# Recurrent gates of an RG-LRU layer: three products of 64 rows each in place of two products of 128 stacked rows

## The chip, the cores and the metric

The kernel runs on one NeuronCore of a Trainium2 chip. TensorE (PE) multiplies matrices and writes PSUM. VectorE (DVE), ScalarE (ACT) and GpSimd (POOL) do elementwise work, and SyncE (SP) issues most transfers. The metric is the device time of one execution in microseconds (us), lower is better, and it is given as the median of several runs. For the kernel before it is 686.44 us, the median of 3 runs from 683.94 to 686.56.

## The reference, cut to what matters

One encoder layer on x of shape (1, 1024, 1024), float32: an input LayerNorm, one wide input projection, neighbourhood attention, a bidirectional RG-LRU recurrence, gated merging of the two branches, an output projection, and a last LayerNorm. The change is in the gates of the recurrence. There, `w_gate` holds one 64 x 64 matrix for each of 8 channel blocks and each of the two gates r and i, and each of the two directions has its own set.

```python
u = centred_depthwise_conv(u, conv_w, conv_b)                 # (1, 1024, 512)
h = rg_lru(u, gate_w[0], gate_b[0], lam[0], False) + rg_lru(u, gate_w[1], gate_b[1], lam[1], True)

def rg_lru(x, w_gate, b_gate, lam, reverse):
    xb = x.reshape(B, S, N_BLOCKS_B, BLOCK_W)                 # 8 blocks x 64
    g = jnp.einsum('bsnd,gnde->gbsne', xb, w_gate) + b_gate[:, None, None]
    g = jax.nn.sigmoid(g.astype(jnp.float32)).reshape(2, B, S, W)
    r_gate, i_gate = g[0], g[1]
    log_a = -C_LRU * jax.nn.softplus(-lam.astype(jnp.float32)) * r_gate
    a = jnp.exp(log_a)
    ...
    bx = mult * i_gate * x.astype(jnp.float32)
    _, h = lax.associative_scan(_lin_combine, (a, bx), axis=1, reverse=reverse)
```

## The kernel before

**Split precision.** Matmul operands are in the type float32r. To keep float32 accuracy, an operand f is split into a high part (`hi`, f cast to float32r) and a low part (`lo = f - hi`, `lo_of`, line 119). A product is then the sum of high x high, low x high and high x low (`mm3`, line 122): three matmuls, each with its own weight load.

**The stages.** After LayerNorm, the v and q projections, the main loop (line 973) runs over slots: 16 pairs of column tiles of the input projection, 7 slots for each pair, 116 slots with the tail. `product(p, k)` puts one slot's 24 multiplications of a Strassen-like scheme on TensorE: 128 x 128 weights, 128 x 512 moving data. In about the 145th to the 372nd us the recurrence is laid into this loop. Attention follows, then the merge and the output projection.

**Who sets the order.** The order on all engines is the program order: TensorE's is written by hand, and `tc.manual_schedule` (line 141) fixes that of the other four. Within a slot, work registered with `at(slot, 0, f)` is issued before `product`, and that of `at(slot, 1, f)` after it. `CONV_AT` (line 32) gives the first slot of each of the 4 channel tiles' convolution, `GATE_AT` (line 33) that of each of the 8 gate stages (channel tile t, direction d).

**The convolution stage** (`conv_stage`, line 675) makes a channel tile's `uc`: 128 channels, which are two blocks of 64, by 1024 positions. It also loads that tile's gate weights (`w_gate`, line 681), casts them (`weights`, line 700, ACT) and makes their low part (`weights_lo`, line 704, POOL). `split(b)` and `split_lo(b)` (lines 689 and 695) build one stacked operand for each block b: in `us[b]` one half of the 128 rows is the high part of the block's 64 channels (ACT), and the other half their low part (DVE). The host lays the 64 weight rows of a block out twice, once for each half.

**The gate stage** (`gate_stage`, line 718). `gates(b)` (line 721) makes both gates of block b over all 1024 positions, 64 output columns each: for each of the two halves of the positions one matmul with the high weights and one with the low weights. As the rows are stacked, these two give all four products of high and low parts. So a stage has 8 matmuls, and the 8 stages have 64. The result fills `o`, two PSUM banks, one for each half of the positions; the pool `psd` has one such buffer, so that `gates(1)`, two slots later, writes where the sigmoids of `gates(0)` have read. `sigmoid(b, c)` (line 732, ACT) reads 64 x 1024 from PSUM, two for each `gates` call, one slot after it. Then follow the gated input on POOL (line 739), exp, tanh, square and root on ACT, the scan on DVE.

Of the kernel before, what the change touches and what calls it, by code (L numbers as in the profile page):

```python
# [9 lines left out]
F32 = mybir.dt.float32  # L10
F32R = mybir.dt.float32r
AF = mybir.ActivationFunctionType
ALU = mybir.AluOpType

P = 128
S = 1024
# [6 lines left out]
HALF = 512  # L23
# [23 lines left out]
HALVES = ((slice(0, 64), slice(64, P)), (slice(64, P), slice(0, 64)))  # L47
# [8 lines left out]
def tiled(ap, n):  # L56

    return ap[:, n * HALF:(n + 1) * HALF].rearrange("p (j r c) -> p j r c", r=GR, c=8)


def gridded(ap, n):

    return ap.rearrange("p (r j c) -> p j r c", r=GR, c=8)[:, 4 * n:4 * n + 4]
# [3 lines left out]
def encoder_kernel(ctx, tc, x, gb1, gb, w_qk, w_v, w_s, w_ba, w_bb, w_gate, smalls, bias, w_out, out):  # L67
    nc = tc.nc
    V, A, G, PE, SP = nc.vector, nc.scalar, nc.gpsimd, nc.tensor, nc.sync

    def pool(name, side="left", **kw):
        return tc.alloc_tile_pool(name=name, bufs=1, side=side, reuse_waits="tile", **kw)
# [11 lines left out]
    def bank(name):  # L84
        return banks[0].tile([P, HALF], F32, tag="bank", name=name)
# [21 lines left out]
    sm = cst.tile([P, SM_N], F32, name="sm")  # L107

    def pair(pl, shape, name, **kw):
        return [pl.tile(shape, F32R, name=f"{name}_{c}", **({**kw, "tag": kw["tag"] + c} if "tag" in kw else kw))  # L110
                for c in "hl"]
# [7 lines left out]
    def lo_of(eng, lo, full, hi):  # L119
        eng.tensor_tensor(lo, full, hi.bitcast(F32), ALU.subtract)  # L120
# [70 lines left out]
    halves = [slice(c * HALF, (c + 1) * HALF) for c in range(2)]  # L191
# [394 lines left out]
    psd = tc.alloc_tile_pool(name="psd", bufs=1, space=bass.MemoryType.PSUM, reuse_waits="tile")  # L586
# [3 lines left out]
    ev = pool("ev", "right")  # L590
    lru = pool("lru", "right")
# [22 lines left out]
    ups, ucs, hsum = {}, {}, {}  # L614
# [57 lines left out]
    def at(slot, pos, f):  # L672
        todo.setdefault((slot, pos), []).append(f)

    def conv_stage(t, slot):
        cw = SM_CW + 4 * t

        def begin():
            uc = lru.tile([P, S], F32, tag="uc", bufs=2, name=f"uc{t}")
            gs = ev.tile([P, 4, P], F32, tag="z", bufs=5, name=f"gw{t}")  # L680
            SP.dma_start(gs[:], w_gate[t])
            ucs[t] = [uc, [None, None], None, gs]
            A.activation(uc[:], ups[t][:, 0:S], AF.Identity, bias=sm[:, SM_CB + t:SM_CB + t + 1], scale=sm[:, cw:cw + 1])

        def tap(j):
            uc = ucs[t][0]
            V.scalar_tensor_tensor(uc[:], ups[t][:, j:j + S], sm[:, cw + j:cw + j + 1], uc[:], ALU.mult, ALU.add)  # L687

        def split(b):
            uc, us = ucs[t][:2]  # L690
            own, other = HALVES[b]
            us[b] = lru.tile([P, S], F32R, tag=f"us{b}", name=f"us{t}_{b}")
            A.copy(us[b][own], uc[own])

        def split_lo(b):
            uc, us = ucs[t][:2]
            own, other = HALVES[b]
            lo_of(V, us[b][other], uc[own], us[b][own])

        def weights():  # L700
            gw = ucs[t][2] = pair(lru, [P, 4, P], f"gw{t}", tag="gw")
            A.copy(gw[0][:], ucs[t][3][:])

        def weights_lo():
            hi, lo = ucs[t][2]
            lo_of(G, lo[:], ucs[t][3][:], hi[:])

        at(slot, 1, begin)
        for j in range(1, 4):
            at(slot + j, 1, lambda j=j: tap(j))  # L710
        at(slot + 2, 1, weights)
        at(slot + 3, 1, weights_lo)
        at(slot + 5, 1, lambda: split(0))
        at(slot + 6, 0, lambda: split_lo(0))
        at(slot + 6, 1, lambda: split(1))
        at(slot + 7, 0, lambda: split_lo(1))

    def gate_stage(t, d, slot):
        g = {}

        def gates(b):
            uc, us, gw, _ = ucs[t]
            if b == 0:
                for c in "ria":
                    g[c] = lru.tile([P, S], F32, tag=c, name=f"{c}{t}_{d}")
            o = psd.tile([P, 2, HALF], F32, tag="gates", name=f"g{t}{d}{b}")
            for n in range(2):
                for z, w in enumerate(gw):
                    PE.matmul(o[:, n, :], w[:, 2 * d + b, :], us[b][:, n * HALF:(n + 1) * HALF], start=z == 0, stop=z == 1)  # L729
            g["o"] = o[:].rearrange("p n f -> p (n f)")  # L730

        def sigmoid(b, c):
            own, other = HALVES[b]
            src = own if c == "r" else other
            col = SM_GB + (d * 2 + b) * 4 + t
            A.activation(g[c][own], g["o"][src], AF.Sigmoid, bias=sm[src, col:col + 1])

        def gated_input():
            G.tensor_tensor(g["i"][:], g["i"][:], ucs[t][0][:], ALU.mult)

        def decay():
            A.activation(g["a"][:], g["r"][:], AF.Exp, scale=nsp[:, d * 4 + t:d * 4 + t + 1])

        def growth():
            w = g["w"] = lru.tile([P, S], F32, tag="wh", bufs=2, name=f"w{t}_{d}")
            A.activation(w[:], g["r"][:], AF.Tanh, scale=sp[:, d * 4 + t:d * 4 + t + 1])

        def square():
            A.activation(g["r"][:], g["a"][:], AF.Square)

        def left():
            V.scalar_tensor_tensor(g["w"][:], g["r"][:], 1.0, g["w"][:], ALU.add, ALU.mult)

        def root():
            A.activation(g["w"][:], g["w"][:], AF.Sqrt)

        def tables():
            A.activation(warm[:], eps_t[:], AF.Sigmoid)

        def inputs():  # L760
            first = S - 1 if d else 0
            V.memset(g["w"][:, first:first + 1], 1.0)
            G.tensor_tensor(g["w"][:], g["i"][:], g["w"][:], ALU.mult)

        def scan():
            st = -1 if d else 1
            w = g["w"]
            V.tensor_tensor_scan(w[:, ::st], g["a"][:, ::st], w[:, ::st], 0.0, ALU.mult, ALU.add)
            if d == 0:
                hsum[t] = w  # L770

        def fetch():
            for n in range(2):
                zs = g["out", n] = ev.tile([P, HALF], F32, tag="z", bufs=5, name=f"zs{t}_{n}")
                SP.dma_start(zs[:], zb_d[t][:, n * HALF:(n + 1) * HALF])

        def total():
            V.tensor_tensor(hsum[t][:], g["w"][:], hsum[t][:], ALU.add)

        def gated(n):  # L780
            zs = g["out", n]
            V.tensor_tensor(tiled(zs[:], 0), gridded(hsum[t][:], n), tiled(zs[:], 0), ALU.mult)
            SP.dma_start(yb_d[t][:, n * HALF:(n + 1) * HALF], zs[:])

        for b in range(2):
            at(slot + 2 * b, 1, lambda b=b: gates(b))
            for c in "ri":
                at(slot + 2 * b + 1, 1, lambda b=b, c=c: sigmoid(b, c))
        at(slot + 4, 0, gated_input)
        at(slot + 4, 1, decay)  # L790
        at(slot + 5, 1, growth)
        at(slot + 6, 1, square)
        at(slot + 7, 1, left)
        at(slot + 8, 1, root)
        at(slot + 9, 0, tables)
        at(slot + 9, 0, inputs)
        at(slot + 10, 1, scan)
        if d:
            at(slot + 10, 1, fetch)
            at(slot + 11, 1, total)  # L800
            for n in range(2):
                at(slot + 12 + n, 0, lambda n=n: gated(n))
# [74 lines left out]
    for t, slot in enumerate(CONV_AT):  # L877
        conv_stage(t, slot)
    for n, slot in enumerate(GATE_AT):
        gate_stage(n // 2, n % 2, slot)  # L880
# [92 lines left out]
    for slot in range(7 * N_PAIR + 4):  # L973
        p, k = divmod(slot, 7)
# [44 lines left out]
    vvs, sums, scs, tps, pts, attns, rsb, gates = {}, {}, {}, {}, {}, {}, {}, {}  # L1019
# [125 lines left out]
    for unit in range(-NT, H * NT + PV_LAG):  # L1145
        h, c = divmod(unit, NT)
        before, b = divmod(unit - 1, NT)
# [83 lines left out]
    for slot in range(2 * NK + 2):  # L1231
        j, n = divmod(slot, 2)
# [12 lines left out]
        if j < NK:  # L1245
# [3 lines left out]
            o = sums_m[slot] = pst.tile([P, HALF], F32, tag="mb", bufs=2, name=f"mb0{n}") if slot < 2 else bank(f"mb{j}{n}")  # L1249
# [32 lines left out]
    def o_product(i, cols):  # L1282
        o = bank(f"o{i}_{cols.start}")
        w = cols.stop - cols.start
        run(mm3(o[:, :w], [([t[k, i // 4][:, ti(i)] for t in (mh, ml)], [t[:, cols] for t in wo[k]])
                           for k in range(NK)]))
        return o[:, :w]
# [19 lines left out]
    for i in range(NT):  # L1307
        last = i == NT - 1
        load_z(i + 3)
        z = zs.pop(i)  # L1310
# [3 lines left out]
        for cols in [halves[0]] + (pieces[2:] if last else [halves[1]]):  # L1314
            o = o_product(i, cols)
# [110 lines left out]
```

## Time and profile before

| what | value |
|---|---|
| median of 3 runs | 686.44 us (683.94 to 686.56) |
| the profiled execution, its own time | 684.15 us |
| its span, first to last instruction | 682.4 us |
| mean granted TensorE clock | 0.996 |
| HBM read, written | 77.11 MB, 35.68 MB |

The profile shows one execution. A row of a group of instructions has the line in the kernel, the engine, the operation, output and inputs by the program's names, the shape, the count, the busy time in us and the mean of one in ns, and at its end the engine's idle time ahead of these instructions with what ended most of it. PE is the matmul, PEld the weight load, which overlaps it. The end of a matmul is modelled, so its duration is longer than the distance from its start to the next one's start; that distance is called its pitch below. In shapes, 128*64 would be 128 rows by 64 columns of weights, and 128x512 is the moving data.

### The profile page before, as it was taken

How to read it: one execution, taken by the hardware profiler on the slowest of the kernel's cores; microseconds unless marked ns; L12 is line 12 of the kernel's file. 1: busy time of each engine (PE TensorE's matmuls, PEld its weight loads, DVE VectorE, ACT ScalarE, POOL GpSimd, SP SyncE). 2: the span in 40 equal slices, each digit the busy share in tenths (PEclk: the TensorE clock that was granted, in tenths of full speed). 3: DMA queues.
4: the chain of work that ended last, by engine and by line, in shares of the span. 5: the costliest groups of instructions: out<-in, count | busy, mean ns of one | idle time of the engine just before them, and what ended most of it. 6: DMA issues, size and time to landing. Idle time of an engine off the chain costs nothing.

```text
span 682.4 us, 9299 instructions
## 1 busy us (share of the span) xinstructions
PE 666.3 (98%) x3177; PEld 555.0 (81%) x3177; DVE 495.0 (73%) x821; ACT 364.0 (53%) x612; POOL 353.8 (52%) x258
## 2 busy tenths in 40 slices
PE   8999999999999999999999999999999999999995
PEld 6787888888888888888788888888888878888884
DVE  7866766796899599879977785377788777533434
ACT  4553524247686677768576635477777544310110
POOL 5697451344576577567647534115255446435442
PEclk9999999999999999999999999999999999999998
DMA  8754164233424133531453457898794557512211
GB/s 314 241 187 154 63 233 169 78 92 124 124 93 147 68 109 110 183 124 47 170 198 114 174 175 262 293 371 304 257 322 141 179 192 279 183 62 93 92 62 61
DMA packets 48702, 113.39 MB, mean 166 GB/s; under 512 B 5056, under 2 KB 9744, under 8 KB 47120
## 3 DMA queue, kind: packets, MB, share of 16 engines
q1 hardware_dynamic: 48624, 112.81, 47.6%
q8 instruction: 25, 0.41, 0.2%
q14 instruction: 21, 0.17, 0.1%
q10 hardware_dynamic: 32, 0.01, 0.0%
HBM read 77.11 MB, written 35.68 MB: 165 GB/s over the span
## 4 chain that ended last, share of the span: by engine, by line
PE 81%; DVE 8%; DMA 4%; POOL 3%; ACT 1%; issue 1%; SPq 1%; DVEq 0%; POOLq 0%; ACTq 0%
PE a L126 29%; PE o L126 13%; PE s L126 11%; PE mb L126 10%; PE q L126 5%; PE acc L1077 3%; PE s L1031 3%; PE pt L1053 2%; POOL x L238 2%; PE v L303 2%; PE g L729 2%; DMA wvsl<-in_w_v_dram 1%; DMA ks<-k_d 1%; DVE ws_l L120 1%; DVE uc L687 1%
## 5 line engine op out<-in xcount | busy, mean ns | idle before, releaser
L126 PE MATMUL o<-wo_h,ml 128*128 128x512 f32 (+1 forms) x136 | 51.2, 377 | 0.0
L126 PE MATMUL o<-wo_l,mh 128*128 128x512 f32 (+1 forms) x136 | 51.2, 376 | 0.0
L126 PE MATMUL o<-wo_h,mh 128*128 128x512 f32 (+1 forms) x136 | 51.2, 376 | 0.0
L126 PE MATMUL a<-ht_h,ws_h 128*128 128x512 f32 x128 | 50.0, 390 | 0.0
L126 PE MATMUL a<-ht_h,ws_l 128*128 128x512 f32 x128 | 49.8, 389 | 0.0
L126 PE MATMUL a<-ht_l,ws_h 128*128 128x512 f32 x128 | 49.8, 389 | 0.0
L126 PE MATMUL a<-b_h,wa_h 128*128 128x512 f32 x128 | 49.8, 389 | 0.0
L126 PE MATMUL a<-b_h,wa_l 128*128 128x512 f32 x128 | 49.8, 389 | 0.0
L126 PE MATMUL a<-b_l,wa_h 128*128 128x512 f32 x128 | 49.8, 389 | 0.0
L1041 DVE CUSTOM_DVE_ANT_0 sc<-s,bias 128x384 f32<-128x384 f32 (+1 forms) x64 | 33.4, 522 | 22.4 <-PE s L1031 14.0
L1316 DVE SCALAR_TENSOR_TENSOR z<-z,o 128x512 f32<-128x512 f32 (+1 forms) x17 | 11.2, 656 | 51.1 <-PE o L126 51.1
L1061 ACT CAST pt_h<-pt 128x384 fp32r<-128x384 f32 x64 | 29.0, 454 | 25.8 <-PE pt L1053 17.9
L1326 POOL TENSOR_TENSOR z<-z,gb 128x1024 f32<-128x1024 f32 x7 | 16.8, 2396 | 48.7 <-ACT z L1325 48.7
L1046 ACT ACTIVATE p<-sc,summ 128x384 f32<-128x384 f32 (+1 forms) x64 | 37.8, 591 | 5.2 <-DVE summ L1041 5.0
L1295 ACT ACTIVATE sd<-mv,eps_z 128x1 f32<-128x1 f32 x8 | 2.4, 294 | 67.1 <-DVE mv L1321 67.1
L303 PE MATMUL v<-wv,b_h 128*128 128x512 f32 x128 | 32.8, 398 | 2.7 <-ACT b_h L258 1.6
L120 DVE TENSOR_TENSOR pt_l<-pt,pt_h 128x384 fp32r<-128x384 f32 x64 | 33.2, 519 | 2.1 <-ACT pt_h L1061 1.6
L1031 PE MATMUL s<-ks,qs 128*128 128x384 f32 (+1 forms) x128 | 31.3, 326 | 0.5 <-DMA ks<-k_d 0.5
L837 POOL CAST wb_h<-wb 128x512 fp32r<-128x512 f32 x9 | 7.0, 780 | 47.5 <-DMA wb<-in_w_bb_dram 29.6
L303 PEld LDWEIGHTS v<-wv,b_h 128*128 128x128 f32 x128 | 23.6, 188 | 9.2 <-ACT b_h L258 2.3
L120 POOL TENSOR_TENSOR wb_l<-wb,wb_h 128x512 fp32r<-128x512 f32 x16 | 22.2, 1388 | 16.4 <-ACT wb_h L835 15.6
L1053 PEld LDWEIGHTS pt<-ident,p 128*128 128x128 f32 x176 | 23.1, 140 | 8.6
(438 smaller groups left out, 2201.3 us busy)
## 6 DMA issues: line engine op xcount, KB each, us to landing
ks<-k_d SPq DMA_DIRECT2D x8, 1024.0 KB, 8.0
h_d<-x SPq DMA_DIRECT2D x8, 512.0 KB, 4.5
v_d<-vs SPq DMA_DIRECT2D x8, 512.0 KB, 4.0
q_d<-q SPq DMA_DIRECT2D x8, 512.0 KB, 3.0
ga_d<-ga SPq DMA_DIRECT2D x16, 256.0 KB, 2.0
gb_d<-gb SPq DMA_DIRECT2D x16, 256.0 KB, 2.1
k_d<-k SPq DMA_DIRECT2D x8, 512.0 KB, 4.0
qs<-q_d SPq DMA_DIRECT2D x8, 512.0 KB, 5.5
```

The source lines that it names most:

```text
L120: eng.tensor_tensor(lo, full, hi.bitcast(F32), ALU.subtract)
L126: PE.matmul(o, a, b, start=first and i == 0, stop=last and i == len(prods) - 1, skip_group_check=not (first and last))
L238: G.tensor_tensor(z[:, halves[c]], z[:, halves[c]], gb_t[w][c][:], op)
L303: PE.matmul(vos[i][:], a, wv[kind == "w"][k][:], start=vn[i] == 0, stop=vn[i] == 23)
L729: PE.matmul(o[:, n, :], w[:, 2 * d + b, :], us[b][:, n * HALF:(n + 1) * HALF], start=z == 0, stop=z == 1)
L1031: PE.matmul(o[:, :P * len(near(t))], q[:, t * P:(t + 1) * P], k[:, z, keys], start=z == 0, stop=z == 1)
L1041: V.tensor_tensor_reduce(s[:, :w], o[:, :w], heads[h][2][:, b0:b0 + w], -1.0, 3.0e38, ALU.add, ALU.min, accum_out=sums[h][0][:, t:t + 1])
L1046: A.activation(probs[h % 2][t][:], scs.pop((h, t))[:, :w], AF.Exp, bias=sums[h][0][:, t:t + 1], scale=-1.0, accum_out=sums[h][1][:, t:t + 1])
L1053: PE.transpose(tp[:, n * P:(n + 1) * P], probs[h % 2][t][:, z * P:(z + 1) * P], ident[:])
L1061: A.copy(pt[0][:, span(b)], tps[h, b][:, :P * len(near(b))])
L1077: PE.matmul(acc[g][:, d:d + w], vvs[h // 2][:, b, h % 2, :], pt[:, a:a + w], start=b in (1, 6) and z == 0, stop=z == 1 and b == (4, 7)[g])
L1326: G.tensor_tensor(z[:], z[:], gb2[:, 0, :], ALU.mult)
```

## The change

The kernel before has two operands of 128 stacked rows for a channel tile, one for each block. After the change, the operands are the high and the low part of the whole `uc`, in place: rows 0 to 63 are block 0, rows 64 to 127 block 1. A `gates(n)` call now makes both blocks over half n of the positions. It has three products (high weights x high data, high x low, low x high), and for each of them two matmuls in turn, one on rows 0 to 63 for block 0 and one on rows 64 to 127 for block 1. Each has 64 rows, 128 columns of weights and 512 columns of moving data, and writes the PSUM bank of its block. A stage has 12 such matmuls, and the 8 stages have 96. The product of the two low parts is no longer computed.

The high part takes one cast for a channel tile in place of two, the low part one subtraction in place of two. The gate weights are no longer laid out twice, so their tile halves from 128 x 512 to 128 x 256. A sigmoid now covers 64 rows by 512 positions, and there are four after each `gates` call.

```diff
         def begin():
             ...
-            gs = ev.tile([P, 4, P], F32, tag="z", bufs=5, name=f"gw{t}")
+            gs = ev.tile([P, 2, P], F32, tag="z", bufs=5, name=f"gw{t}")
             SP.dma_start(gs[:], w_gate[t])
...
-        def split(b):
-            uc, us = ucs[t][:2]
-            own, other = HALVES[b]
-            us[b] = lru.tile([P, S], F32R, tag=f"us{b}", name=f"us{t}_{b}")
-            A.copy(us[b][own], uc[own])
-
-        def split_lo(b):
-            uc, us = ucs[t][:2]
-            own, other = HALVES[b]
-            lo_of(V, us[b][other], uc[own], us[b][own])
+        def split():
+            us = ucs[t][1] = [lru.tile([P, S], F32R, tag=f"us{c}", name=f"us{t}_{c}") for c in "hl"]
+            A.copy(us[0][:], ucs[t][0][:])
+
+        def split_lo():
+            hi, lo = ucs[t][1]
+            lo_of(V, lo[:], ucs[t][0][:], hi[:])

         def weights():
-            gw = ucs[t][2] = pair(lru, [P, 4, P], f"gw{t}", tag="gw")
+            gw = ucs[t][2] = pair(lru, [P, 2, P], f"gw{t}", tag="gw")
             A.copy(gw[0][:], ucs[t][3][:])
...
-        at(slot + 5, 1, lambda: split(0))
-        at(slot + 6, 0, lambda: split_lo(0))
-        at(slot + 6, 1, lambda: split(1))
-        at(slot + 7, 0, lambda: split_lo(1))
+        at(slot + 5, 1, split)
+        at(slot + 6, 0, split_lo)
...
-        def gates(b):
-            uc, us, gw, _ = ucs[t]
-            if b == 0:
+        def gates(n):
+            uc, (uh, ul), (wh, wl), _ = ucs[t]
+            if n == 0:
                 for c in "ria":
                     g[c] = lru.tile([P, S], F32, tag=c, name=f"{c}{t}_{d}")
-            o = psd.tile([P, 2, HALF], F32, tag="gates", name=f"g{t}{d}{b}")
-            for n in range(2):
-                for z, w in enumerate(gw):
-                    PE.matmul(o[:, n, :], w[:, 2 * d + b, :], us[b][:, n * HALF:(n + 1) * HALF], start=z == 0, stop=z == 1)
-            g["o"] = o[:].rearrange("p n f -> p (n f)")
-
-        def sigmoid(b, c):
+            o = g["o"] = psd.tile([P, 2, HALF], F32, tag="gates", name=f"g{t}{d}{n}")
+            for z, (w, u) in enumerate(((wh, uh), (wh, ul), (wl, uh))):
+                for b in range(2):
+                    own = HALVES[b][0]
+                    PE.matmul(o[:, b, :], w[own, d, :], u[own, halves[n]], start=z == 0, stop=z == 2)
+
+        def sigmoid(n, b, c):
             own, other = HALVES[b]
             src = own if c == "r" else other
             col = SM_GB + (d * 2 + b) * 4 + t
-            A.activation(g[c][own], g["o"][src], AF.Sigmoid, bias=sm[src, col:col + 1])
+            A.activation(g[c][own, halves[n]], g["o"][src, b, :], AF.Sigmoid, bias=sm[src, col:col + 1])
...
-        for b in range(2):
-            at(slot + 2 * b, 1, lambda b=b: gates(b))
-            for c in "ri":
-                at(slot + 2 * b + 1, 1, lambda b=b, c=c: sigmoid(b, c))
+        for n in range(2):
+            at(slot + 2 * n, 1, lambda n=n: gates(n))
+            for b, c in ((0, "r"), (1, "r"), (0, "i"), (1, "i")):
+                at(slot + 2 * n + 1, 1, lambda n=n, b=b, c=c: sigmoid(n, b, c))
...
-    gates = np.concatenate([gw, gw], axis=3).transpose(1, 3, 0, 2, 4).reshape(4, P, 4, P)
+    gates = gw.transpose(1, 2, 3, 0, 4).reshape(4, P, 2, P)
```

More of the change, by code (lines that the diff above doesn't have):

```diff
@@ L679, in begin @@
             uc = lru.tile([P, S], F32, tag="uc", bufs=2, name=f"uc{t}")
-            gs = ev.tile([P, 4, P], F32, tag="z", bufs=5, name=f"gw{t}")
+            gs = ev.tile([P, 2, P], F32, tag="z", bufs=5, name=f"gw{t}")
             SP.dma_start(gs[:], w_gate[t])
-            ucs[t] = [uc, [None, None], None, gs]
+            ucs[t] = [uc, None, None, gs]
             A.activation(uc[:], ups[t][:, 0:S], AF.Identity, bias=sm[:, SM_CB + t:SM_CB + t + 1], scale=sm[:, cw:cw + 1])
```

## The prediction, made before the changed kernel ran

> **What bounds the kernel now.** First the page's head, the waits of PE in the stretch that holds the gates, and that stretch's busy times (columns: stretch, its length, then busy time and instructions of each engine, granted clock, DMA share, GB/s).
>
> ```profile
> span 682.4 us, 9299 instructions
> PE 666.3 (98%) x3177; PEld 555.0 (81%) x3177; DVE 495.0 (73%) x821; ACT 364.0 (53%) x612; POOL 353.8 (52%) x258
> ...
> PE a L126 <- DVE w L762: 0.4, 1, 0.4
> ...
> 128.00:400.00 272.00, 271.63 (x1196) 223.74 (x1195) 231.26 (x241) 184.03 (x231) 162.95 (x114) 1.00 0.36 121
> ```
>
> PE is busy for 271.63 of 272.00 us, at the full granted clock, and in all that time it waits once, 0.4 us. DVE with 231.26 us and ACT with 184.03 have room. As modelled ends hide small gaps, the timeline of PE is needed too: the first matmuls of `gates(0)` and `gates(1)` of the first gate stage, with the 24 of `product` between them.
>
> ```profile
> 150.30 0.39 PE L126 MATMUL a<-b_l,wa_h 128*128 128x512 f32 x1
> 150.53 0.39 PE L729 MATMUL g<-us,gw_h 128*128 128x512 f32 x1
> ...
> 151.43 0.39 PE L126 MATMUL a<-b_h,wa_h 128*128 128x512 f32 x1
> ...
> 156.87 0.39 PE L729 MATMUL g<-us,gw_h 128*128 128x512 f32 x1
> ```
>
> From 150.53 to 156.87 us there are 28 matmuls, so the pitch is 6.34 / 28 = 0.2264 us, though each is shown as lasting 0.39. Over the whole stretch, 1196 x 0.2264 = 270.8 of 272 us. So here time is the number of matmuls times the pitch, and what changes on PE lands in the end time one to one, while what changes on other engines lands nowhere until PE has to wait.
>
> **The change on PE.** The instructions that it replaces, from the view of the tile g (count, then duration in ns: least, median, most):
>
> ```profile
> L729 PEld LDWEIGHTS g<-us,gw_h x32: 187/188/188, 150.3 to 369.7; 128*128 128x128 f32 x32
> L729 PE MATMUL g<-us,gw_h x32: 389/389/389, 150.5 to 369.9; 128*128 128x512 f32 x32
> ...
> L729 PE MATMUL g<-us,gw_l x32: 388/389/389, 150.8 to 370.1; 128*128 128x512 f32 x32
> ```
>
> It removes 32 + 32 = 64 matmuls: 64 x 0.2264 = 14.5 us of PE. It adds 8 stages x 12 = 96 of 64 rows with the same 512 columns. What one of these costs has no row, as no matmul of 64 rows is in the trace. It is bounded from both sides.
>
> The upper bound is that each takes a whole pitch. Fewer rows alone shorten nothing, as the only instruction with few rows shows, 16 of 128:
>
> ```profile
> L383 PEld LDWEIGHTS clock<-ident,gb_row x1: 177/177/177, 3.1 to 3.1; 16*128 16x128 f32 x1
> ```
>
> Its load takes 177 ns, that of 128 rows 188. Then the 96 take 96 x 0.2264 = 21.7 us, and the change costs 32 x 0.2264 = +7.2 us.
>
> The lower bound is that the two of a pair, on rows 0 to 63 and 64 to 127 and into different PSUM banks, run side by side. A pair takes at least one pitch, since the next matmul on the same rows has to follow with its 512 columns. Then 48 pairs take 48 x 0.2264 = 10.9 us: 16 pitches less, -3.6 us. What could prevent that even where the halves are independent is the rate of loads, two in a pitch. Here the trace speaks, in the transposes of attention with the products behind them; the first part has a matmul with 8 columns of weights (128*8) among them, the second has none:
>
> ```profile
> 446.09 0.49 PE L1053 MATMUL pt<-ident,p 128*128 128x128 f32 x3
> 446.42 0.27 PE L1096 MATMUL pt<-ident,sums 128*8 128x128 f32 x1
> 446.42 0.19 PEld L1077 LDWEIGHTS acc<-pt_h,vv 128*128 128x128 f32 x1
> 446.53 0.19 PEld L1077 LDWEIGHTS acc<-pt_l,vv 128*128 128x128 f32 x1
> 446.77 0.34 PE L1077 MATMUL acc<-pt_l,vv 128*128 128x384 f32 x1
> ...
> 449.38 0.49 PE L1053 MATMUL pt<-ident,p 128*128 128x128 f32 x3
> 449.62 0.48 PE L1077 MATMUL acc<-pt_h,vv 128*128 128x512 f32 x1
> 449.94 0.34 PE L1077 MATMUL acc<-pt_l,vv 128*128 128x384 f32 x1
> ```
>
> Three transposes take (446.42 - 446.09) / 3 = 0.11 us each, weight load included, and two loads start 446.53 - 446.42 = 0.11 us apart although each lasts 0.19. Two loads in a pair are 0.22 us, just under the pitch of 0.2264: they fit, with nothing to spare. If the second half's load trails by that 0.11 us and the next full-array matmul waits for it, each of the 16 calls loses 0.11 us, 1.8 us in all, and the gain shrinks to -1.8.
>
> I take the pairs as overlapping without the trail: between -3.6 and +7.2 the rows that come nearest are those of the loads, which leave room for two instructions in one pitch; and the operands of a pair share neither rows nor PSUM bank. The Trainium skill has a rule on this: by "TensorE: Matmul & The Clock Gate", section "Part 3: Packing small matmuls — row/col tiling", matmuls in different row groups run concurrently, starting about 4 ns apart; by that estimate each call has one such 4 ns, and the term is -3.6 + 16 x 0.004 = -3.5 us. No run shown here has such a pair.
>
> **The switch of shape.** Each `gates` call now stands between products of 128 rows, so PE goes to another shape and back 16 times: 32 switches. With the 128*8 matmul in between, 446.77 - 446.09 = 0.68 us pass; without it 449.94 - 449.38 = 0.56. The difference, 0.12, is the 0.11 of one more transpose plus 0.01 for both switches: 16 x 0.01 = 0.2 us, which I take. That row narrows the columns and not the rows, so I keep an upper bound: a switch that waits until the matmul before it has left the array loses the duration beyond the pitch, 0.389 - 0.2264 = 0.163 us, 32 x 0.163 = 5.2 us. It can't gain anything, as before there is no wait at that place to remove.
>
> **The other engines.** The rows that carry this: the casts and subtractions of the operand, the weights, the sigmoids, and as price of a 512-wide one with a bias the tanh on `ga`.
>
> ```profile
> L693 ACT CAST us<-uc x8: 1037/1046/1058, 142.4 to 319.6; 64x1024 fp32r<-64x1024 f32 x8
> L120 DVE TENSOR_TENSOR us<-uc,us x8: 1218/1221/1602, 146.0 to 322.2; 64x1024 fp32r<-64x1024 f32 x8
> ...
> L702 ACT CAST gw_h<-gw x4: 621/622/624, 132.7 to 308.7; 128x512 fp32r<-128x512 f32 x4
> L120 POOL TENSOR_TENSOR gw_l<-gw,gw_h x4: 1735/2031/2353, 138.5 to 309.4; 128x512 fp32r<-128x512 f32 x4
> ...
> L736 ACT ACTIVATE r<-g,sm x16: 1102/1113/1119, 153.7 to 370.5; 64x1024 f32<-64x1024 f32 x16
> ...
> L642 ACT ACTIVATE ga<-a,smh x8: 689/692/694, 177.5 to 356.1; 128x512 f32<-128x512 f32 x8
> ```
>
> DVE loses 4 of 8 subtractions, 4 x 1.22 = 4.9 us; ACT 4 casts, 4 x 1.05 = 4.2, and at most half of 4 x 0.62; POOL at most half of 4 x 2.03. The weights' four transfers halve. The sigmoids go from 32 x 1.11 = 35.6 us to 64 x 0.69 = 44.2: +8.6, so ACT has about 3 us more in the 272, of which it uses 184. All of this lies beside PE and enters the sum with nothing: PE waited 0.4 us for all of them together, and that is also the most that their relief could give.
>
> One cover is thin. `gates(1)` writes the one PSUM buffer that the sigmoids of `gates(0)` read. In the first stage these run, behind the one table load that they have, at
>
> ```profile
> L736 ACT ACT_TABLE_LOAD  x1: 1283/1283/1283, 152.4 to 152.4; - x1
> ...
> 153.70 1.11 ACT L736 ACTIVATE r<-g,sm 64x1024 f32<-64x1024 f32 x1
> 154.82 1.11 ACT L736 ACTIVATE i<-g,sm 64x1024 f32<-64x1024 f32 x1
> ...
> 214.52 1.12 ACT L736 ACTIVATE i<-g,sm 64x1024 f32<-64x1024 f32 x1
> ...
> 217.94 0.39 PE L729 MATMUL g<-us,gw_h 128*128 128x512 f32 x1
> ```
>
> The first stage's end at 155.93, 0.9 us ahead of 156.87. Four of 0.69 end 0.53 later and still in time. In the other stages there is no table load ahead of them; in the third, the last of the sigmoids ends at 215.64, and the buffer is written again 2.3 us later. Late sigmoids would hold PE, and then all products behind, one to one. The operand of the first gates is ready no later than before: its cast and its subtraction keep their slots, and the removed pair was the later one.
>
> **The sum.** -3.6 + 0.2 = -3.4 us. The profiled execution took 684.15 us by itself (1.75 us beside its span), so 680.7. Of the three runs shown, one (683.94) lies with it, two (686.44, 686.56) lie 2.3 above; on the median, 686.44 - 3.4 = 683.0. I forecast 683.0 us for the median, and hold 680.5 possible for its lower kind of run.
>
> **Rivals.**
>
> *No overlap* (the other side). PE takes the two of a pair one after the other, at the place of the 16 calls. The mechanism decides as soon as a pair takes more than 64 x 0.2264 / 48 = 0.302 us; with a full pitch each it is +7.2: 691.4 on the profile's time, 693.6 on the median. For it speaks that the trace has not one matmul starting while another still feeds 512 columns: behind every 512-wide one in the rows above the next starts a whole pitch later. Against it, that so far each needed all rows.
>
> *Overlap, but each switch waits.* -3.6 + 5.2 = +1.6 us: 685.8 to 688.0. Against it speaks the 0.01 of the 128*8 row. The Trainium skill has this as a rule: by "TensorEngine Tiling (Array Packing)", section "Key Properties", a change of the tiling mode drains TensorE. By that rule the forecast would be this case; the trace shows no drain at the 128*8 matmul, and shows nothing of one in rows.
>
> *Neither overlap nor free switches.* +7.2 + 5.2 = +12.4: 696.6 to 698.8.
>
> **How the numbers follow.** Overlap with switches nearly free 0.52, overlap with waiting switches 0.12, no overlap 0.28, no overlap with waiting switches 0.08. About 0.5% (3.4 us) is what a measurement of this kernel can tell from no change. The forecast lies on that bound; of its 0.52, I give 0.20 to faster and 0.32 to within 0.5%, since every loss that I named (trail, sigmoids) pulls it inward. The waiting switches with overlap are within it (0.12), the other two slower (0.36). So faster 0.20, same 0.44, slower 0.36. The range goes from 684.15 - 3.6 = 680.5 to 694.5, the median with no overlap (693.6) and a little of the second rival's switch cost: it leaves out the last case and holds about 0.9; less can't be left out without losing the 0.28. The forecast's own range is 680.5 to 684.7 (686.56 with the smaller gain of 1.8).
>
> **What would show it.** In the changed profile, the matmuls on g are 96 of 64 rows, 64*128. Between the first of `gates(0)` and of `gates(1)` of the first stage there are 24 products and 6 matmuls: 24 x 0.2264 + 3 x 0.2264 = 6.11 us with overlap, 5.43 + 1.36 = 6.79 without, against 6.34 now. A start-to-start distance inside a pair of a few ns or of 0.11 us is overlap, 0.226 is none. A gap of 0.16 between the last product and the first of 64 rows, or behind the last, is the waiting switch. Idle time of PE put down to ACT r or ACT i would mean that the sigmoids are late. The prediction is wrong if pairs take over 0.3 us, or if PE is found waiting for ACT by more than 1 us in this stretch.

## The result, and the profile after

The changed kernel takes 687.35 us (median of 20 runs, 685.89 to 691.34), the kernel before 685.36 us (20 runs, 683.94 to 687.29). The ratio is 1.0032 with a 95% interval of 1.002 to 1.0044: about 2.2 us slower, within 0.5%. The forecast was 3.4 us faster. Runs of one kernel spread over some 3 us or more: the profiles of e2, e3, e4, e5 and e9 below, all from longer runs of theirs, show a granted clock of 0.94 between 540 and 570 us, far behind the gates, where all others show 1.00.

The head of the page of the changed kernel:

```profile
span 685.1 us, 9387 instructions
PE 667.6 (97%) x3209; PEld 548.7 (80%) x3209; DVE 485.0 (71%) x817; ACT 366.6 (54%) x640; POOL 337.6 (49%) x258
```

Its busy times in the stretch with the gates (columns as before: PE, PEld, DVE, ACT, POOL, clock, DMA):

```profile
128.00:400.00 272.00, 272.00 (x1219) 216.98 (x1218) 218.73 (x235) 186.35 (x259) 144.86 (x112) 1.00 0.35 118
```

PE is busy throughout, as before. DVE has 218.73 us in place of 231.26, POOL 144.86 in place of 162.95, ACT 186.35 in place of 184.03. The view of the tile g shows the new instructions (count, then least, median and most duration in ns):

```profile
L726 PEld LDWEIGHTS g<-us_h,gw_h x32: 182/183/183, 151.0 to 371.7; 64*128 64x128 f32 x32
L726 PE MATMUL g<-us_h,gw_h x32: 493/493/493, 151.0 to 371.8; 64*128 64x512 f32 x32
...
L726 PE MATMUL g<-us_l,gw_h x32: 392/393/394, 151.3 to 372.1; 64*128 64x512 f32 x32
...
L732 ACT ACTIVATE r<-g,sm x32: 672/686/690, 154.1 to 373.5; 64x512 f32<-64x512 f32 x32
```

How they lie on PE is in the timelines of PE and of its weight loads around the first `gates` call ("x2" is two instructions put into one row; "issue" means that the engine waited for nothing that the profile shows):

```profile
150.45 0.39 PE L126 MATMUL a<-b_h,wa_l 128*128 128x512 f32 x1
150.68 0.39 PE L126 MATMUL a<-b_l,wa_h 128*128 128x512 f32 x1
150.99 0.50 PE L726 MATMUL g<-us_h,gw_h 64*128 64x512 f32 x2
151.33 0.40 PE L726 MATMUL g<-us_l,gw_h 64*128 64x512 f32 x2
151.56 0.40 PE L726 MATMUL g<-us_h,gw_l 64*128 64x512 f32 x2
151.89 0.50 PE L126 MATMUL a<-b_h,wa_h 128*128 128x512 f32 x1
152.23 0.40 PE L126 MATMUL a<-b_h,wa_l 128*128 128x512 f32 x1
```

```profile
150.45 0.19 PEld L126 LDWEIGHTS a<-b_l,wa_h 128*128 128x128 f32 x1
150.99 0.19 PEld L726 LDWEIGHTS g<-us_h,gw_h 64*128 64x128 f32 x2 [0.35 <-issue]
151.10 0.19 PEld L726 LDWEIGHTS g<-us_l,gw_h 64*128 64x128 f32 x2
...
151.89 0.19 PEld L126 LDWEIGHTS a<-b_h,wa_h 128*128 128x128 f32 x1 [0.37 <-issue]
152.00 0.19 PEld L126 LDWEIGHTS a<-b_h,wa_l 128*128 128x128 f32 x1
```

Two things are to be seen. The pairs do lie side by side: two matmuls fit into 0.50 us although each lasts 0.49, and all six of a call take 151.89 - 150.99 = 0.90 us, which is 0.15 each, less than a pitch. And at both ends time is lost. In the stream of equal shapes a weight load starts together with the matmul ahead of it (150.45) and is done when its own turn comes. Here the load for the first pair starts only at 150.99, 0.31 us after the last 128-row matmul, so 0.31 - 0.2264 = 0.09 us later than a next matmul would have. Then the step to the second pair is 151.33 - 150.99 = 0.34, another 0.11 more than a pitch, because the load was not ahead. Going back costs the same: 151.89 - 151.56 = 0.33 and 152.23 - 151.89 = 0.34.

From 150.68 to 152.23 us there are 1.55 us for one product matmul, three pairs and one product matmul, 5 pitches or 1.13 us if nothing were lost. So a call loses 0.42 us, 0.2 for each switch. Before, the same place took 6 pitches, 1.36 us. All 16 calls of the trace are within 0.01 us of these 1.55. Each call is 0.19 us longer, 16 calls 3.1 us.

From that, about 1 us comes back. In the trace of before, PE had stalls in this stretch; the largest is in its timeline:

```profile
327.71 0.39 PE L126 MATMUL s<-b_l,ws_h 128*128 128x512 f32 x1
328.47 0.50 PE L126 MATMUL a<-ht_h,wa_h 128*128 128x512 f32 x1 [0.37 <-DVE w L762]
328.81 0.40 PE L126 MATMUL a<-ht_h,wa_l 128*128 128x512 f32 x1
```

The steps are 0.76 and 0.34 in place of 0.2264 each, 0.64 us lost to DVE; with three smaller ones (0.24 at 186.57, 0.08 at 261.50, 0.07 at 322.40) it is about 1.0 us. The profile names DVE for the large one alone; what the small ones waited for it does not say. None of them is in the trace of the changed kernel. 3.1 - 1.0 = 2.1 us, and measured are 2.2 +- 0.8. The two profiles agree: from the first matmul of the first call to that of the last, 150.53 to 369.43 before and 150.99 to 371.75 after, the stretch is 1.86 us longer, for 15 calls x 0.19 = 2.9 less 1.0. The whole spans differ by 2.7 us; of that, 0.46 lies ahead of the first call and 0.38 behind the start of the last.

### The profile page after: what moved, and what is told of

Its sections match the earlier page's. It is cut to its first block, busy times and chain, and to the rows that moved or that the text cites. A ratio compares the mean times of both kernels' runs of the same rounds, so it can differ in the third digit from the quotient of the medians.

```text
span 685.1 us, 9387 instructions
## 1 busy us (share of the span) xinstructions
PE 667.6 (97%) x3209; PEld 548.7 (80%) x3209; DVE 485.0 (71%) x817; ACT 366.6 (54%) x640; POOL 337.6 (49%) x258
## 4 chain that ended last, share of the span: by engine, by line
PE 85%; DVE 4%; DMA 4%; POOL 4%; ACT 1%; issue 1%; SPq 1%; DVEq 0%; POOLq 0%; ACTq 0%
PE a L126 32%; PE s L126 13%; PE o L126 13%; PE mb L126 10%; PE q L126 5%; PE acc L1073 3%; POOL x L238 3%; PE s L1027 3%; PE pt L1049 2%; PE g L726 2%; PE v L303 2%; DMA wvsl<-in_w_v_dram 1%; DMA ks<-k_d 1%; DMA rsb<-rs_d 1%; DVE b_l L120 0%
```

## The experiments

Theory 1 is that reading: the pairs overlap, and each switch between matmuls of 128 and of 64 rows costs about 0.2 us. Its rival, theory 2, is that the loss lies in the pairs, with two weight loads in one pitch, and that a switch is free. Times are medians. The ratio to the kernel before, with its 95% interval, is not the quotient of the two medians and can differ from it by up to 0.0024.

**One small matmul on the kernel before, in three shapes.** It stands ahead of the others in each `gates` call, behind the line that allocates `o`, and its result is overwritten. e1 gives it 64 rows:

```diff
+            PE.matmul(o[:, 0, :64], gw[0][0:64, 2 * d + b, :], us[b][0:64, 0:64], start=True, stop=True)
```

> Kernel before, with one extra small matmul of 64 rows (64*128 weights, 64 columns of moving data) ahead of each of the 16 gates calls; its result is overwritten. Theory 1 (each switch between a 128-row and a 64-row matmul costs about 0.2 us: PE finishes what is running, and the next weight load is not ahead): 0.09 + 0.105 going in, 0.10 + 0.105 coming out and some 0.03 to 0.06 for the small matmul, 16 x 0.45 = about +7 us on the kernel before. Theory 2 (the loss of the changed kernel is in its pairs, two weight loads in one pitch, and a switch is free): one more weight load at a pitch of 0.11 us each, 16 x 0.11 = at most +1.8 us.

Measured: 692.08 us against 685.76 (1.0116, 1.0079 to 1.0153). The timeline of PE at a call of the third gate stage:

```profile
213.08 0.39 PE L126 MATMUL a<-b_l,wa_h 128*128 128x512 f32 x1
213.40 0.29 PE L727 MATMUL g<-us,gw_h 64*128 64x64 f32 x1
213.62 0.50 PE L730 MATMUL g<-us,gw_h 128*128 128x512 f32 x1
213.96 0.39 PE L730 MATMUL g<-us,gw_l 128*128 128x512 f32 x1
```

From the product matmul to the second gate matmul it is 0.88 us where two pitches would be 0.45: the small matmul with its two switches costs 0.43 us. e2 is the control with all rows:

```diff
+            PE.matmul(o[:, 0, :64], gw[0][:, 2 * d + b, :], us[b][:, 0:64], start=True, stop=True)
```

> The control: the same extra small matmul with all 128 rows (128*128 weights, 64 columns of moving data), no switch. Both theories: 16 x 0.11 = at most +1.8 us on the kernel before.

Measured: 688.31 us (1.0053, 1.0033 to 1.0072). The same place in its timeline:

```profile
212.35 0.39 PE L126 MATMUL a<-b_l,wa_h 128*128 128x512 f32 x1
212.58 0.19 PE L727 MATMUL g<-us,gw_h 128*128 128x64 f32 x1
212.61 0.48 PE L730 MATMUL g<-us,gw_h 128*128 128x512 f32 x1
212.92 0.39 PE L730 MATMUL g<-us,gw_l 128*128 128x512 f32 x1
```

That is 0.57 us, 0.12 for the small matmul. e3 has all rows and 64 columns of weights:

```diff
+            PE.matmul(o[0:64, 0, :64], gw[0][:, 2 * d + b, 0:64], us[b][:, 0:64], start=True, stop=True)
```

> The same extra small matmul with 128 rows and 64 columns of weights (128*64). It tells whether the 128*8 row, by which the prediction priced the switch, was misread or only of another kind. If narrowing the columns is no switch for PE: as the control, at most +1.8 us. If each change of shape costs what theory 1 says: about +7 us.

Measured: 689.35 us (1.0062, 1.0038 to 1.0087). Its timeline at that place:

```profile
212.08 0.39 PE L126 MATMUL a<-b_l,wa_h 128*128 128x512 f32 x1
212.30 0.19 PE L727 MATMUL g<-us,gw_h 128*64 128x64 f32 x1
212.33 0.48 PE L730 MATMUL g<-us,gw_h 128*128 128x512 f32 x1
212.65 0.39 PE L730 MATMUL g<-us,gw_l 128*128 128x512 f32 x1
```

Again 0.57 us. So the loss comes with the switch in rows, without any pair, which theory 2 does not have, and narrowing the columns costs nothing like it. e1's 692.08 - 685.76 = 6.3 us (8.0 by the ratio, its interval from 5.4 to 10.5) fits 16 x 0.43 = 6.9.

The times of e2 and e3 come out above the 1.8 us of the expectation, and the interval of e3 overlaps that of e1, so for these the profiles decide. From the first matmul of the first `gates` call to that of the last there are 218.90 us in the kernel before, 220.63 in e2 (151.11 to 371.74), 220.90 in e3 (150.80 to 371.70) and 224.44 in e1 (150.79 to 375.23). That is 1.7 and 2.0 us more for e2 and e3, where 15 x 0.12 would be 1.8, and 5.5 for e1, where 15 x 0.43 is 6.5 and about 0.8 of stalls is gone. What e2's and e3's profiles lose beyond that lies behind the last call: 315.8 and 317.8 us are left there, 312.9 before.

**The loops exchanged.** e4 runs block by block:

```diff
-            for z, (w, u) in enumerate(((wh, uh), (wh, ul), (wl, uh))):
-                for b in range(2):
+            for b in range(2):
+                for z, (w, u) in enumerate(((wh, uh), (wh, ul), (wl, uh))):
```

> Changed kernel with the loops exchanged: three matmuls of block 0, then three of block 1, so that only one neighbouring pair lies on different rows. If the pairs of the changed kernel really run side by side: 5 to 6 pitches for a call in place of 3, so +7.2 to +10.9 us on the changed kernel, +9 to +13 on the kernel before. If the equal starts in the records are only how they are recorded: as the changed kernel, +2 us on the kernel before.

Measured: 686.70 us (1.0041, 1.0019 to 1.0063), as the changed kernel. A miss: the overlap is there in full, though the program has all of block 0 ahead of block 1. Its PE timeline:

```profile
149.97 0.39 PE L126 MATMUL a<-b_l,wa_h 128*128 128x512 f32 x1
150.29 0.50 PE L726 MATMUL g<-us_h,gw_h 64*128 64x512 f32 x2
150.62 0.40 PE L726 MATMUL g<-us_l,gw_h 64*128 64x512 f32 x2
150.86 0.40 PE L726 MATMUL g<-us_h,gw_l 64*128 64x512 f32 x2
151.19 0.50 PE L126 MATMUL a<-b_h,wa_h 128*128 128x512 f32 x1
```

The first row holds the first and the fourth matmul of the call, which have the same operands by name: the fourth starts with the first, and the call takes 0.90 us again. This left open whether the halves run side by side or a 64-row matmul is just fast, which e8 settles.

**Both matmuls of a pair on the same rows.** Block 1's gates are made from block 0's data here.

```diff
-                    own = HALVES[b][0]
-                    PE.matmul(o[:, b, :], w[own, d, :], u[own, halves[n]], start=z == 0, stop=z == 2)
+                    rows = HALVES[0][0]
+                    PE.matmul(o[:, b, :], w[rows, d, :], u[rows, halves[n]], start=z == 0, stop=z == 2)
```

> Changed kernel with both matmuls of a pair on rows 0 to 63, so that block 1's gates are computed from block 0's channels and weights. It tells why six 64-row matmuls fit into 0.9 us, which the exchanged loops did not tell, as the two halves started together there too. If the halves of the rows run side by side, the six now follow one another: 6 pitches in place of 3, 16 x 3 x 0.2264 = +10.9 us on the changed kernel, about +13 on the kernel before. If a 64-row matmul is by itself twice as fast: as the changed kernel, +2 us.

Measured: 698.84 us against 686.01 (1.0191, 1.0166 to 1.0216), +12.8. In the PE timeline the first pair now takes 0.73 us where it took 0.50:

```profile
151.32 0.73 PE L727 MATMUL g<-us_h,gw_h 64*128 64x512 f32 x2
151.89 0.63 PE L727 MATMUL g<-us_l,gw_h 64*128 64x512 f32 x2
152.36 0.62 PE L727 MATMUL g<-us_h,gw_l 64*128 64x512 f32 x2
152.91 0.50 PE L126 MATMUL a<-b_h,wa_h 128*128 128x512 f32 x1
```

The call takes 152.91 - 151.32 = 1.59 us, not 0.90. Matmuls on the same rows follow one another a pitch apart; the overlap is that of the two halves, and it is worth what was worked out.

**Half and double the switches.** e5 puts a stage's 12 matmuls into one call, in which both halves' sums go through the same two banks, one after the other, and the sigmoids of both halves read what is left there.

```diff
+            if n == 1:
+                return
             o = g["o"] = psd.tile([P, 2, HALF], F32, tag="gates", name=f"g{t}{d}{n}")
-            for z, (w, u) in enumerate(((wh, uh), (wh, ul), (wl, uh))):
+            for m in (1, 0):
+                for z, (w, u) in enumerate(((wh, uh), (wh, ul), (wl, uh))):
...
```

> Changed kernel with all 12 matmuls of a gate stage in its first call and none in the second: 16 switches in place of 32, the same matmuls. For that both halves of the positions go through the same two PSUM banks, so the sigmoids of the second half read the sums of the first half. Theory 1: 16 x 0.2 = -3.3 us on the changed kernel, about -1.3 on the kernel before. Theory 2 (loss in the pairs): no difference to the changed kernel.

Measured: 684.82 us against 685.62 (0.9994, 0.9976 to 1.0013), 2.5 us below the changed kernel. Its timeline of PE at the first call:

```profile
150.02 0.39 PE L126 MATMUL a<-b_l,wa_h 128*128 128x512 f32 x1
150.33 0.50 PE L729 MATMUL g<-us_h,gw_h 64*128 64x512 f32 x2
...
151.92 0.50 PE L126 MATMUL a<-b_h,wa_h 128*128 128x512 f32 x1
152.26 0.40 PE L126 MATMUL a<-b_h,wa_l 128*128 128x512 f32 x1
```

From 150.02 to 152.26 us there are one product matmul, six pairs and one product matmul, 8 pitches or 1.81 us, and they take 2.24: 0.43 lost, as with three pairs. e9 moves the first pair of each call ahead of the last three matmuls of the product before it.

```diff
...
-            at(slot + 2 * n, 1, lambda n=n: gates(n))
+            at(slot + 2 * n, 2, lambda n=n: gates(n, 0))
+            at(slot + 2 * n, 1, lambda n=n: gates(n, 1))
...
+        for i, _ in enumerate(steps):
+            if i == 8:
+                for f in todo.pop((slot, 2), ()):
+                    f()
```

> Changed kernel with the first pair of each call moved ahead of the last three matmuls of the product in front of it: the same matmuls, 64 switches in place of 32. Theory 1: 32 x 0.2 = +6.4 us on the changed kernel, about +8.4 on the kernel before. Theory 2 (loss in the pairs): no difference to the changed kernel.

Measured: 696.95 us against 686.01 (1.0138, 1.0104 to 1.0172), +9.5 by the ratio, its interval from 7.1 to 11.8. Both move as theory 1 says, where theory 2 has no difference. In e9's timeline of PE a call looks like this:

```profile
213.83 0.39 PE L126 MATMUL a<-b_l,wa_h 128*128 128x512 f32 x1
214.15 0.50 PE L727 MATMUL g<-us_h,gw_h 64*128 64x512 f32 x2
214.58 0.50 PE L126 MATMUL a<-b_h,wa_h 128*128 128x512 f32 x1
214.92 0.39 PE L126 MATMUL a<-b_h,wa_l 128*128 128x512 f32 x1
215.15 0.40 PE L126 MATMUL a<-b_l,wa_h 128*128 128x512 f32 x1
215.48 0.50 PE L727 MATMUL g<-us_l,gw_h 64*128 64x512 f32 x2
```

A single pair between two switches takes 0.32 + 0.43 + 0.34 us from the product matmul ahead of it to the second one behind, 0.41 above three pitches: the price belongs to the visit, whatever its length. From the first pair of the first call to that of the last, e9's profile takes 227.28 us (150.62 to 377.90) and that of the changed kernel 220.76: 6.5 us more, for 15 x 0.41 = 6.2 and one wait of PE for ACT of 0.2. Not all of e9's time is due to the switches: behind its last gates call its profile takes 3.6 us more than that of the changed kernel.

**The relief of DVE.** e6, on the changed kernel, makes the parts of `uc` in two pieces of 64 rows again.

```diff
...
-        at(slot + 5, 1, split)
-        at(slot + 6, 0, split_lo)
+        at(slot + 5, 1, lambda: split(0))
+        at(slot + 6, 0, lambda: split_lo(0))
+        at(slot + 6, 1, lambda: split(1))
+        at(slot + 6 + (t > 0), 1 - (t > 0), lambda: split_lo(1))
```

> Changed kernel with the high and low parts of uc made in two pieces of 64 rows again: DVE and ACT get back 4 x 1.2 and 4 x 1.05 us, PE stays as it is. If the relief of DVE is what removed the stalls of PE that the kernel before has in this stretch (0.24 + 0.08 + 0.07 + 0.64 = 1.0 us): up to +1.0 us on the changed kernel. If these stalls come and go by chance: 0.

Measured: 687.37 us against 685.62 (1.0035, 1.0019 to 1.0052), no difference to the changed kernel that the runs could tell. Its timeline of PE has the stall back, at the same matmul of the program:

```profile
330.15 0.39 PE L126 MATMUL s<-b_l,ws_h 128*128 128x512 f32 x1
330.81 0.50 PE L126 MATMUL a<-ht_h,wa_h 128*128 128x512 f32 x1 [0.28 <-DVE w L763]
331.15 0.39 PE L126 MATMUL a<-ht_h,wa_l 128*128 128x512 f32 x1
```

It is 0.66 + 0.34 - 0.45 = 0.55 us, so that part of the 1.0 us is seen to hang on DVE's load, in one profile each and not in the times. The three small stalls are not back. Less work on DVE is also not the only thing that removes the large one: in e1, with DVE's work as before, PE comes to the same matmul 4.6 us later (333.06 in place of 328.47) and the step ahead of it is 0.23 us. e7, on the kernel before, moves one low part of each tile from DVE to POOL.

```diff
-            lo_of(V, us[b][other], uc[own], us[b][own])
+            lo_of(G if b else V, us[b][other], uc[own], us[b][own])
```

> Kernel before with the low part of each tile's second block made on POOL and not on DVE: DVE has 4 x 1.2 us less, PE and its matmuls are untouched. If the relief of DVE is worth 1.0 us: down to -1.0 us on the kernel before, a version faster than both. If not, or if POOL gets late with it: 0 or slower.

Measured: 688.70 us (1.0049, 1.0031 to 1.0066), 3.4 slower by the ratio. Why is in the waits of PE in this stretch (total us, times, longest)

```profile
PE a L126 <- DVE w L762: 3.0, 3, 1.4
```

and in its view of the tile us:

```profile
L120 DVE TENSOR_TENSOR us<-uc,us x4: 1220/1598/1602, 145.1 to 320.8; 64x1024 fp32r<-64x1024 f32 x4
L120 POOL TENSOR_TENSOR us<-uc,us x4: 2717/2724/3422, 145.2 to 323.0; 64x1024 fp32r<-64x1024 f32 x4
```

POOL takes 2.72 us for what DVE did in 1.22, the median of DVE's remaining four went from 1.22 to 1.60, and PE waited for DVE three times, 3.0 us. So this is no way to keep the relief without the switches.

No version was clearly faster than the kernel before. e5's order would need the sums of both halves to live at once, four PSUM banks; the gates have two and the products the other six. That was not tried, as e5's interval includes no difference at all.

## Why the prediction was wrong, point by point

**PE sets the time in this stretch: right.** It is busy for 272.00 of 272.00 us after, and the difference of 1.86 us between the two stretches is made up of PE's steps: the switches, less the stalls. (The description of the kernel before gives one slot's product 24 multiplications. It has 12; the 24 between the two calls of a stage, which the prediction counts, are those of two slots.)

**The pairs overlap without a trail: right.** Loads two to a pitch do fit; the steps inside a call are 0.23 to 0.24 us behind the first. e8 shows the worth of it: +12.8 us without the overlap against +2.2 with it, where 10.9 were worked out. The Trainium skill's page "TensorE: Matmul & The Clock Gate", section "Part 3: Packing small matmuls — row/col tiling", agrees so far: matmuls in different row groups run concurrently, here a pair in 0.50 us where each lasts 0.49. Its statement there that matmuls start in program order does not fit the trace of e4, in which the fourth of a call starts with the first.

**The price of a switch: this step failed.** It read "446.77 - 446.09 = 0.68 us pass; without it 449.94 - 449.38 = 0.56" and took "16 x 0.01 = 0.2 us". That row narrows the columns, and e3 shows that this costs no more than any small matmul, so the row was read rightly and was the wrong row. The switch in rows costs 0.2 us, 16 x 0.42 = 6.7 us in all. The upper bound of 0.163 each was too low as well: it held only the wait for the matmul that is running, and not that the next weight load can't go ahead meanwhile. The wait is in fact smaller, 0.09 to 0.10, and the load adds 0.11. The trace of before had that second part to show, at 328.47: after a stall the step to the next matmul is 0.34 us too. With 6.7 in place of 0.2 the prediction's sum is -3.6 + 6.7 = +3.1 us, and about 1.0 us of stalls less makes it +2.1. The distance that it named as a sign, from the first gates matmul of the first call to that of the second, came out at 157.55 - 150.99 = 6.56 us: its 6.11 with overlap, 0.42 for one visit, and 0.03.

**The second rival was what happened.** It gave overlap with waiting switches +1.6 us, 685.8 to 688.0, with a chance of 0.12. Its mechanism holds; that its number came so near was partly luck, as its 5.2 us for the switches was 1.5 too low and the stalls that went, 1.0 us, were not in it. The page "TensorEngine Tiling (Array Packing)" of the Trainium skill, section "Key Properties", has the rule, that changing the tiling mode drains TensorE. For the rows the trace agrees, with 0.2 us a switch; for the columns e3 shows no such cost, 0.57 us as in e2, though this rule of the Trainium skill excepts no direction. The prediction weighed a row in the columns above this rule.

**The other engines: mostly right.** The 512-wide sigmoids take 0.686 us where 0.69 was priced, ACT has 186.35 us, and PE never waits for it in this stretch. The relief of DVE was held to be worth 0.4 us at most, by the waits. The steps of PE show about 1.0 us of stalls before, more than the one wait of 0.4 that is listed, and they are gone after; that is what made the loss 2 us and not 3. That DVE's relief removed them is seen for 0.55 us of it, by e6; for the rest it is open. Over the whole execution DVE has 10.0 us less (495.0 to 485.0) and POOL 16.2 (353.8 to 337.6), where 4.9 and at most 4.1 were priced: instructions whose work did not change got shorter too, and no run here says why.

## What to carry to other kernels

Two 64-row matmuls on the two halves of the rows cost one pitch, but a visit to that shape in a stream of 128-row matmuls cost 0.42 us here, about 1.8 pitches of 512 columns. Count the pitches that one visit saves: this change saved one (lost 0.19 us each time), e5 two (about even); by this count only visits that save three or more would pay clearly, which no run here tried. For a price that the trace lacks, take a row that changes the same thing, rows for rows, and if there is none, give the drain and the unhidden weight load each their term.

## What the hardware showed that was not expected

The two halves of the rows did not keep program order between them: in e4, three matmuls of block 0 ahead of three of block 1 gave the same call of 0.90 us as the pairs in turn, with the fourth starting beside the first; in program order, it could not have started before the third, two steps (0.57 us) later. And a switch in rows is costly (0.43 us for one small 64-row matmul, in and out), while the same small matmul with half of the columns costs the 0.12 us of one with all of them.
